# A hybrid attention and mixture-of-experts block: rotary dimensions gathered in one tile of q and one of k, and POOL's large operations given to DVE

## The chip, the cores and the metric

The kernel runs on one core of a Trainium2 chip. The metric is the device time of one execution in microseconds. In the profile the engines are PE (matrix products), PEld (loading their stationary operands), DVE (vector), ACT (scalar), POOL (GpSimd) and SP, which here only issues transfers.

## The reference

One encoder layer over 1024 tokens of width 1024, in float32. The part that the change touches is the input projection of the first sub-layer:

```python
mod = jax.nn.silu(c) @ w_ada[l] + b_ada[l]
sh1, sc1, g1, sh2, sc2, g2 = jnp.split(mod, N_MOD, axis=-1)
h = rms_norm(x, norm1_g[l]) * (1.0 + sc1[:, None]) + sh1[:, None]
z = h @ w_in[l]
q = z[..., :A].reshape(B, S, N_DIFF_HEADS, 2, DIFF_HEAD_DIM)
k = z[..., A:2 * A].reshape(B, S, N_DIFF_HEADS, 2, DIFF_HEAD_DIM)
v = z[..., 2 * A:3 * A].reshape(B, S, N_DIFF_HEADS, DIFF_VALUE_DIM)
u = z[..., 3 * A:].reshape(B, S, N_POOL_GROUPS, POOL_GROUP_DIM)
a_out = diff_attention(q, k, v, lam, subln_g[l], lambda_init)
p_out = multiscale_pool(u, w_pool[l], pool_scale[l])
```

A is 512, and there are four heads with two components of 64 dimensions each, so eight components for q and eight for k. In each component the first 16 dimensions are rotated: the first 8 and the next 8 are paired, t1·cos − t2·sin and t2·cos + t1·sin. The other 48 pass unchanged. q is scaled by 0.125. `multiscale_pool` takes means over windows of 2, 4, 8 and 16 tokens, one for each group of 128 channels, subtracts the input, and multiplies by a 128x128 matrix. After this sub-layer come a second norm, routing to 2 of 32 experts, the experts, a gated residual and a final norm.

## The kernel before

Activations lie transposed: channels on the 128 partitions, the 1024 tokens along the row. A **slab** is a 128x1024 float32 buffer; 50 of them go round (`slab`). Every precise product is made of three float32r products, high·high, low·high and high·low (`mm3`), so each operand is split: ACT writes the high half (`AF.Copy` to float32r), and DVE or POOL writes the low half as operand minus high (`split`). Nearly all instructions go through one helper line, L82, so they are told apart by tile names. All engines run in program order; the order is that in which the code is written.

The stage around the change is the projection, some 244 us of the span. It does, interleaved:

- `norm1`, `norm1_high`, `norm1_rest`, `norm1_low` for the 8 row blocks k of x: multiply by the root (`xt`), apply scale and shift on ACT (`hh` and `xt`), low half `hl`.
- `wa_sum` and `mod_row`: 48 products of a 128x1024 slab of the modulation weights (`wt`) with the vector `cB`, summed along the row, on DVE.
- 16 projection tiles in the order of ORDER, 48 matrix products of 128x512 each (`pz_q`, `pz_k`, `pz_v`, `pz_u`, in `project`). Tiles 0 to 2 are computed together, block by block, as `hh` and `hl` come (`project3`); tiles 3 to 15 follow one after another. The loop over m runs, for each tile: load weights two tiles ahead (`win`), split those one tile ahead (`wih` on ACT, `wil` on DVE), project, hand the result to a generator (`rope`, `pool_mix`, `values`), take up to three more `mod_row`, and from m = 7 split one slab of the output projection (`wo`, `woh`). `run_later` moves the generators of earlier tiles on by a step.
- `rope` for the four q and four k tiles, one per head: ACT takes the tile from PSUM (`zq`, `zk`), DVE swaps the 8-row halves (`zp`), then two products with `rope_c` and `rope_s`, a sum and the split, on POOL, except for the first product and the split of q0 and k0. The halves go to DRAM (`qd`, `kd`).
- `pool_mix` for the four u tiles: ACT takes the tile (`ub`), POOL makes the running sums (`us`, and on both row ends `ends`), DVE corrects the ends and subtracts, PE multiplies (`py`), ACT and DVE split (`muh`, `mul`).
- from tile 12 on, the first scores of the attention (`s`), their row maxima (`mx`) and exponentials (`e`), before the tile's own products.

PSUM for the tiles is a ring of two 128x1024 buffers (`pt`, tag "p"), which the scores share. SP issues the transfers in order; each waits also for the transfer issued eight before it. `stack_load` brings a head's q and k back, each half stacked as the products want it, at m = 9 and 10 for head 0, and in `attend` for heads 1 to 3.

Of the kernel before, what the change touches and what calls it, by code (L numbers as in the profile page):

```python
# [29 lines left out]
PAD = 8  # L30
# [5 lines left out]
SQ_MAX = float(np.finfo(np.float32).max) * TINY ** 2  # L36
LOAD = 28
AHEAD = 4
ORDER = ["q0", "k0", "v0", "q1", "k1", "u3", "v1", "u2", "q2", "k2", "u1", "q3", "k3", "u0", "v2", "v3"]
START = 12  # L40
STEP = "S0 T0 P0 d1 x1 H0 M0 O L C D0 X0 S1 T1 P1 H1 M1 o Q"
LOADS = {n: 1 for n in range(20, 30)}
# [7 lines left out]
ROWS = [5, 8, 11, 13]  # L50
MODS = {0: 1, 1: 2, 2: 2, **{m: 3 for m in range(3, 12)}}
WO = 7
ROPE = {"q0": "cl", "k0": "cl"}
STACK = (9, 10, 14)
FIRST = (16 - START) // 2
ML = 6
# [12 lines left out]
def block_kernel(ctx: ExitStack, tc: tile.TileContext, A):  # L69
# [4 lines left out]
    dram = ctx.enter_context(tc.tile_pool(name="dram", bufs=1, space=bass.MemoryType.DRAM))  # L74
# [27 lines left out]
    def dma(dst, src):  # L102
        tc.keep_in_program_order(nc.sync.dma_start(dst, src))
# [47 lines left out]
    xt = []  # L151
    for k in range(KD):
        t = slab(f"xt{k}")
# [27 lines left out]
                       allow_small_or_imprecise_dtypes=True)  # L181
    wr = cst.tile([P, KD, 36], F32, name="wr")

    qd = dram.tile([NH, 2, P, S], F32, name="qd")
    kd = dram.tile([NH, 2, P, S], F32, name="kd")
    vd = dram.tile([NH, 2, P, S], F32, name="vd")
    mxd = dram.tile([2, 2, 2, P, 2, 512], F32, name="mxd")
    wod = dram.tile([KD, 2, P, D], F32, name="wod")
# [22 lines left out]
    with tc.tile_pool(name="ps0", bufs=2, space=PSUM) as psum, tc.tile_pool(name="ps1", bufs=2, space=PSUM) as psum1, \  # L211
# [64 lines left out]
        for k in range(KD):  # L276
            sq = slab(f"sq{k}") if k else ssq
# [21 lines left out]
        prs = rows(pt("prs"), r8)  # L299
        rstd = slab("rstd")  # L300
        wa_sum(1, 0)
        w_split(0, pool)
        wa_add(0)
        wa_sum(1, 1)
        act.activation(rstd, prs, AF.Copy)
# [2 lines left out]
        hh, hl = [], []  # L308

        def norm1(k):  # L310
            (pool if k % 2 else dve).tensor_tensor(xt[k], xt[k], rstd, op=OP.mult)

        def norm1_high(k):
            hh.append(slab(f"hh{k}", dt=F32R))
# [4 lines left out]

        def norm1_low(k):  # L320
            hl.append(slab(f"hl{k}", dt=F32R))
            (pool if k % 2 else dve).tensor_tensor(hl[k], xt[k], f(hh[k]), op=OP.subtract)

        rope_c, rope_s = slab("rope_c"), slab("rope_s")
        wpe = slab("wpe", (576,))
# [17 lines left out]
                if 1 in parts:  # L343
                    pe.matmul(PZ[m][h], hi[:, k], hl[k][:, cs], start=False, stop=(k == KD - 1))

        shuf = [(i + 8) % 16 if i < 16 else i for i in range(32)]

        def pool_mix(g, pz):

            w = WINDOWS[g]  # L350
            cur = u = slab(f"ub{g}")
            act.activation(u, pz, AF.Copy)
            ends = sm("ends", (2, 16 + PAD))
            pool.memset(ends, 0.0)
            for i, c in enumerate((0, S - 16)):
                pool.tensor_copy(ends[:, i, PAD - PAD * i:16 + PAD - PAD * i], u[:, c:c + 16])
            lo, hi, size, n = 0, 0, 1, 0
            while size < w:
                a, b = max(1, size // 2), size // 2
                lo, hi = lo + a, hi + b  # L360
                nx, ne = slab(f"us{g}_{n}"), sm("ends", (2, 16 + PAD))
                for y, x, e in ((nx, cur, S - hi), (ne, ends, 16 + PAD - hi)):
                    pool_tt(y[..., lo:e], x[..., lo - a:e - a], x[..., lo + b:e + b], OP.add)
                cur, ends, size, n = nx, ne, size * 2, n + 1
            yield
            yield
# [12 lines left out]
            yield
            for x, t in enumerate((hi, lo)):  # L380
                for a in range(2):
                    dma(mxd[x, a, g // 2, :, g % 2], f(t[:, a * 512:(a + 1) * 512]))

        def rope(nm, pz):
            h = int(nm[1])
            z = slab("z" + nm)
            act.activation(z, pz, AF.Copy, scale=0.125 if nm[0] == "q" else 1.0)
            zp = slab("zp_" + nm)
            dve.stream_shuffle(zp, z, shuf)
            (dve if "c" in ROPE.get(nm, "") else pool).tensor_tensor(z, z, rope_c, op=OP.mult)  # L390
            pool_tt(zp, zp, rope_s, OP.mult)
            pool_tt(z, z, zp, OP.add)
            yield
            hi, lo = slab("th" + nm, dt=F32R), z.bitcast(F32R)
            split(z, hi, lo, None if "l" in ROPE.get(nm, "") else pool)
            yield
            for x, t in enumerate((hi, lo)):
                if nm[0] == "k":
                    dma(kd[h, x], f(t))
                else:  # L400
                    for j in range(2):
                        dma(qd[h, j, 64 * x:64 * x + 64], f(t[64 * j:64 * j + 64]))
# [90 lines left out]
        def stack_load(h, part):  # L493

            q, k1, k2, v = ST.setdefault(h, ([], [], [], []))
            if part == 2:
                for x in range(2):
                    v.append(slab(f"v{x}_{h}", (T, P), F32R))
                    dma(f(v[x].rearrange("p a b -> p (a b)")), vd[h, x])
                return  # L500
            q.append(slab(f"sq{h}_{part}", dt=F32R))
            dma(f(q[-1]), qd[h, part])
            for lab, dst, x in (("k1", k1, 0), ("k2", k2, 1)):
                dst.append(slab(f"{lab}_{h}_{part}", dt=F32R))
                for c in range(2):
                    dma(f(dst[-1][64 * c:64 * c + 64]), kd[h, x, 64 * part:64 * part + 64])

        SUM, MXS, E, WT, PW, SQ, SS8, MX = ({} for _ in range(8))
        Y8 = cst.tile([P, NH, T], F32, name="Y8")
# [170 lines left out]
                    for h in range(2):  # L680
                        project(m, h, (k,), (lo,))

        for k in (0, 1, 3):
            norm1(k)
        w_split(1)
        for k in range(KD):
            if k > 1:
                wa_add(k)
            norm1_high(k)
            if k == 1:  # L690
                w_split(2)
            norm1_rest(k)
            for n in {0: (2,), 1: (3,), 2: (4, 5), 4: (6, 7)}.get(k, ()):
                wa_sum(n, 0)
                wa_sum(n, 1)
            norm1_low(k)
            if k + 2 + 2 * (k % 2) < KD:
                norm1(k + 2 + 2 * (k % 2))
            if k == 0:
                project3(0, (0, 1))  # L700
            elif k == 1:
                project3(0, (2,))
            if k:
                project3(k, (0, 1, 2))
            if k >= 6:
                w_split(k - 3)
        done = 0
        for m, nm in enumerate(ORDER):
# [15 lines left out]
                project(m, 1, range(KD))  # L724
            pz = PZ.pop(m)
            pz = PF[m] if m != 2 else pz
            g = {"u": pool_mix, "v": values}[nm[0]](int(nm[1]), pz) if nm[0] in "uv" else rope(nm, pz)
            next(g, None)
            if m == 15:
                combine(FIRST - 1)  # L730
# [532 lines left out]
def _layouts(inp):  # L1263
    g = {k: np.asarray(v) for k, v in inp.items()}
    a = {}
# [71 lines left out]
```

## Time and profile before

| | |
|---|---|
| median of 3 runs | 1204.95 us (1195.96 to 1205.28) |
| profiled execution | 1198.64 us, span of the trace 1196.9 us |
| busy | PE 1105.3 us (92% of the span), DVE 1014.7, ACT 732.4, POOL 396.8 |
| transfers | 349.60 MB, mean 292 GB/s |

The profiled execution lies within the three runs, 6.3 us below their median. Times of the trace are counted from the start of its span. A PE that is busy is not always a PE at full speed: the granted clock stands beside it in the windows.

### The profile page before, as it was taken

To read this page: it belongs to the slowest core of one execution; us is meant where nothing else is said; L and a number is where in the kernel's file an instruction comes from. 1 tells how busy PE (TensorE), PEld (TensorE's weight loads), DVE (VectorE), ACT (ScalarE), POOL (GpSimd) and SP (SyncE) were. 2 spreads that over 40 slices of the span, in tenths; PEclk is the share of its full clock that TensorE was granted. 3 is DMA by queue.
4 is the path that set the end of the run, shared out by engine and by line. 5 is a ranking of instruction groups with operands and counts; after the bars stand their busy time and mean duration, and the time that the engine had idled before them with its cause. 6 is when DMAs were issued, how large, how long until landed. Compare 5 with 4: busy or idle time off the path is not lost.

```text
span 1196.9 us, 15760 instructions
## 1 busy us (share of the span) xinstructions
PE 1105.3 (92%) x5319; PEld 903.4 (75%) x5319; DVE 1014.7 (85%) x1187; ACT 732.4 (61%) x937; POOL 396.8 (33%) x260
## 2 busy tenths in 40 slices
PE   6696989899999999988999999999999999999975
PEld 6485866677888887777788888888888888888742
DVE  5969898868999725899899999999999999999927
ACT  5443222248888600222788888888888888888812
POOL 3546977737888600343111011011111111101001
PEclk8698999899999999977999999999999999999988
DMA  9836499489563784566699999999999999999155
GB/s 369 314 116 241 125 397 323 174 296 278 136 188 108 299 312 161 164 243 245 197 363 380 383 380 391 392 388 387 384 386 384 388 382 384 384 387 380 46 211 220
DMA packets 102950, 349.60 MB, mean 292 GB/s; under 512 B 15986, under 2 KB 16914, under 8 KB 102866
## 3 DMA queue, kind: packets, MB, share of 16 engines
q1 hardware_dynamic: 91266, 323.08, 73.9%
q0 software_dynamic: 11456, 24.96, 5.6%
q8 instruction: 43, 0.70, 0.2%
q10 hardware_dynamic: 144, 0.52, 0.1%
q14 instruction: 41, 0.34, 0.1%
HBM read 309.95 MB, written 55.33 MB: 305 GB/s over the span
## 4 chain that ended last, share of the span: by engine, by line
issue 46%; PE 26%; DVE 16%; POOL 6%; DMA 4%; ACT 1%; SPq 0%; POOLq 0%; DVEq 0%; ACTq 0%
PE pm L82 7%; PE s L82 4%; DVE wt L82 4%; PE po L82 4%; POOL x L82 4%; PE pz_v L82 3%; POOL yd L82 2%; PE pz_u L82 2%; PE pw L82 2%; DVE rt L82 2%; DMA wt<-in_w_ada 2%; DVE fy L82 1%; PE yp L82 1%; DVE wil L82 1%; DVE xn L82 1%
## 5 line engine op out<-in xcount | busy, mean ns | idle before, releaser
L82 DVE TENSOR_TENSOR wl<-we,wh 128x1024 fp32r<-128x1024 f32 x384 | 458.4, 1222 | 39.6 <-ACT wh L82 34.4
L82 ACT ACTIVATE wh<-we 128x1024 fp32r<-128x1024 f32 x384 | 399.7, 1058 | 60.5 <-PE pg L82 29.0
L82 PE MATMUL pg<-wh,xs 128*128 128x512 f32 x1024 | 338.8, 397 | 0.0
L82 PEld LDWEIGHTS pg<-wh,xs 128*128 128x128 f32 x1024 | 192.8, 188 | 39.1 <-ACT xs L82 0.2
L82 PE MATMUL pg<-wl,xs 128*128 128x512 f32 x512 | 200.0, 391 | 0.0
L82 POOL DMA_INDIRECT yd<-y,ix x32 | 32.1, 1004 | 479.6 <-ACT y L82 466.9
L82 PE MATMUL py<-wh,hth 128*128 128x512 f32 x512 | 171.9, 397 | 1.0 <-ACT hth L82 0.7
L82 PEld LDWEIGHTS py<-wh,hth 128*128 128x128 f32 x512 | 96.1, 188 | 21.8 <-DVE hth L82 1.2
L82 PEld LDWEIGHTS pg<-wl,xs 128*128 128x128 f32 x512 | 96.7, 189 | 18.2
L82 PE MATMUL py<-wl,hth 128*128 128x512 f32 x256 | 99.9, 390 | 0.0
L82 ACT ACTIVATE e<-s,mx 128x1024 f32<-128x1024 f32 x64 | 71.6, 1119 | 42.6 <-DVE mx L82 40.3
L82 DVE SCALAR_TENSOR_TENSOR wt<-wt,cB 128x1024 f32<-128x1024 f32 x48 | 91.1, 1943 | 0.8 <-ACT cB L82 0.8
L82 PE MATMUL s<-k,sq 128*128 128x512 f32 x256 | 74.0, 412 | 10.4 <-ACT e L82 10.3
L82 DVE TENSOR_REDUCE mx<-s 128x1 f32<-128x1024 f32 x64 | 78.2, 1221 | 6.0 <-PE s L82 3.2
L82 POOL TENSOR_TENSOR e<-e,e 128x1024 f32<-128x1024 f32 x32 | 76.5, 2390 | 2.7
L82 PE MATMUL po<-wh,v 128*128 128x256 f32 x256 | 60.7, 301 | 0.0
L82 PEld LDWEIGHTS s<-k,sq 128*128 128x128 f32 x256 | 44.8, 193 | 19.6 <-ACT e L82 13.1
L82 POOL DMA_INDIRECT x<-xnd,ix x32 | 46.2, 1442 | 35.3 <-PE px L82 13.6
L82 PEld LDWEIGHTS py<-wl,hth 128*128 128x128 f32 x256 | 48.2, 188 | 9.4
L82 ACT ACTIVATE xn<-x 128x1024 f32<-128x1024 f32 x7 | 7.4, 1062 | 74.1 <-DVE x L82 68.8
L82 POOL TENSOR_SCALAR e<-e,cc 128x1024 f32<-128x1024 f32 x32 | 39.2, 1225 | 37.2 <-DVE cc L82 16.7
L82 DVE SCALAR_TENSOR_TENSOR x<-pm,Y,x 128x1024 f32<-128x1024 f32 (+1 forms) x33 | 41.2, 1249 | 7.8 <-PE pm L82 6.0
(227 smaller groups left out, 2035.8 us busy)
## 6 DMA issues: line engine op xcount, KB each, us to landing
we<-in_w_exp SPq DMA_DIRECT2D x384, 512.0 KB, 6.9
wt<-in_w_ada SPq DMA_DIRECT2D x48, 512.0 KB, 8.7
win<-in_w_in SPq DMA_DIRECT2D x16, 512.0 KB, 9.1
k<-kd SPq DMA_DIRECT2D x32, 256.0 KB, 9.4
woB<-wod SPq DMA_DIRECT2D x16, 512.0 KB, 6.0
fy<-yd SPq DMA_DIRECT2D x16, 512.0 KB, 10.1
xt<-in_xT SPq DMA_DIRECT2D x8, 512.0 KB, 7.7
wo<-in_w_out SPq DMA_DIRECT2D x8, 512.0 KB, 6.6
```

The source lines that it names most:

```text
L82: ins = getattr(self.eng, op)(*args, **kw)
```

## The change

The columns of w_in are put in another order on the host: the 16 rotated dimensions of all eight components of q make one tile, `qr`, those of k another, `kr`, and the 48 others of each component fill three tiles each (`q0` to `q2`, `k0` to `k2`). `rope` runs for `qr` and `kr` alone, all on DVE. The other six go through a new generator, `plain`, which splits them straight from PSUM. What POOL did in `norm1`, `norm1_low`, `w_split(0)` and `pool_mix` goes to DVE; POOL keeps one small memset for each u tile. `stack_load` puts a component together from 16 rows of one tile and 48 of others. The number of matrix products is the same.

```diff
-ORDER = ["q0", "k0", "v0", "q1", "k1", "u3", "v1", "u2", "q2", "k2", "u1", "q3", "k3", "u0", "v2", "v3"]
+ORDER = ["qr", "kr", "v0", "q0", "k0", "u3", "v1", "u2", "q1", "k1", "u1", "q2", "k2", "u0", "v2", "v3"]
+ROT = 16
...
         def norm1(k):
-            (pool if k % 2 else dve).tensor_tensor(xt[k], xt[k], rstd, op=OP.mult)
+            dve.tensor_tensor(xt[k], xt[k], rstd, op=OP.mult)
...
-            (pool if k % 2 else dve).tensor_tensor(hl[k], xt[k], f(hh[k]), op=OP.subtract)
+            dve.tensor_tensor(hl[k], xt[k], f(hh[k]), op=OP.subtract)
...
-                    pool_tt(y[..., lo:e], x[..., lo - a:e - a], x[..., lo + b:e + b], OP.add)
+                    dve.tensor_tensor(y[..., lo:e], x[..., lo - a:e - a], x[..., lo + b:e + b], op=OP.add)
...
+        def qk_store(nm, hi, lo):
+
+            d, i = (qd if nm[0] == "q" else kd), 0 if nm[1] == "r" else 1 + int(nm[1])
+            for x, t in enumerate((hi, lo)):
+                dma(d[x, i], f(t))
+
         def rope(nm, pz):
...
-            (dve if "c" in ROPE.get(nm, "") else pool).tensor_tensor(z, z, rope_c, op=OP.mult)
-            pool_tt(zp, zp, rope_s, OP.mult)
-            pool_tt(z, z, zp, OP.add)
+            dve.tensor_tensor(z, z, rope_c, op=OP.mult)
+            dve.tensor_tensor(zp, zp, rope_s, op=OP.mult)
+            dve.tensor_tensor(z, z, zp, op=OP.add)
             yield
             hi, lo = slab("th" + nm, dt=F32R), z.bitcast(F32R)
-            split(z, hi, lo, None if "l" in ROPE.get(nm, "") else pool)
...
+            split(z, hi, lo)
+            yield
+            qk_store(nm, hi, lo)
+
+        def plain(nm, pz):
+
+            hi, lo = slab("th" + nm, dt=F32R), slab("tl" + nm, dt=F32R)
+            if nm[0] == "q":
+                act.activation(hi, pz, AF.Copy, scale=0.125)
+                dve.scalar_tensor_tensor(lo, pz, 0.125, f(hi), op0=OP.mult, op1=OP.subtract)
+            else:
+                split(pz, hi, lo)
...
-            q.append(slab(f"sq{h}_{part}", dt=F32R))
-            dma(f(q[-1]), qd[h, part])
-            for lab, dst, x in (("k1", k1, 0), ("k2", k2, 1)):
-                dst.append(slab(f"{lab}_{h}_{part}", dt=F32R))
-                for c in range(2):
-                    dma(f(dst[-1][64 * c:64 * c + 64]), kd[h, x, 64 * part:64 * part + 64])
+            c = 2 * h + part
+            for lab, dst, d, xs in (("sq", q, qd, (0, 1)), ("k1", k1, kd, (0, 0)), ("k2", k2, kd, (1, 1))):
+                t = slab(f"{lab}{h}_{part}", dt=F32R)
+                dst.append(t)
+                for i, x in enumerate(xs):
+                    r = d[x].rearrange("a p s -> (a p) s")
+                    dma(f(t[64 * i:64 * i + ROT]), r[ROT * c:ROT * c + ROT])
+                    n = P + (64 - ROT) * c
+                    dma(f(t[64 * i + ROT:64 * i + 64]), r[n:n + 64 - ROT])
```

Three places show how the order on the engines moves. First DVE at the start of the stage, from the first normalised block (`xt_72` is block 0, `xt_74` block 1, `hl_304` or `hl_303` the low half of block 0; the numbers only tell buffers apart). Before:

```order
L82 TENSOR_TENSOR xt_72<-xt_72,rstd 128x1024
L82 TENSOR_TENSOR wil_296<-win_154,wih_295 128x1024
L82 SCALAR_TENSOR_TENSOR wt_2_156,gs<-wt_2_156,cB 128x1024
L82 SCALAR_TENSOR_TENSOR wt_2_158,sh<-wt_2_158,cB 128x1024
L82 TENSOR_TENSOR hl_304<-xt_72,hh_299 128x1024
L82 TENSOR_TENSOR xt_76<-xt_76,rstd 128x1024
L82 TENSOR_TENSOR wil_324<-win_160,wih_323 128x1024
```

After:

```order
L82 TENSOR_TENSOR xt_72<-xt_72,rstd 128x1024
L82 TENSOR_TENSOR xt_74<-xt_74,rstd 128x1024
L82 TENSOR_TENSOR wil_295<-win_154,wih_294 128x1024
L82 SCALAR_TENSOR_TENSOR wt_2_156,gs<-wt_2_156,cB 128x1024
L82 SCALAR_TENSOR_TENSOR wt_2_158,sh<-wt_2_158,cB 128x1024
L82 TENSOR_TENSOR hl_303<-xt_72,hh_298 128x1024
L82 TENSOR_TENSOR xt_76<-xt_76,rstd 128x1024
L82 TENSOR_TENSOR wil_323<-win_160,wih_322 128x1024
L82 SCALAR_TENSOR_TENSOR wt_3_252,gs<-wt_3_252,cB 128x1024
L82 SCALAR_TENSOR_TENSOR wt_3_254,sh<-wt_3_254,cB 128x1024
L82 TENSOR_TENSOR hl_329<-xt_74,hh_320 128x1024
L82 TENSOR_TENSOR xt_78<-xt_78,rstd 128x1024
```

Each odd block's product and low half, which stood on POOL, now stand between DVE's own.

Second DVE between the low halves of the weights of tile 6 and of tile 7, around tile 5 (`u3`). Before, to the weights of tile 7 (`wil_840`):

```order
L82 TENSOR_TENSOR wil_746<-win_661,wih_745 128x1024
L82 SCALAR_TENSOR_TENSOR wt_3_653,mcol<-wt_3_653,cB 128x1024
L82 SCALAR_TENSOR_TENSOR wt_4_656,mcol<-wt_4_656,cB 128x1024
L82 SCALAR_TENSOR_TENSOR wt_5_659,mcol<-wt_5_659,cB 128x1024
L82 TENSOR_TENSOR mcol<-mcol,cols 128x8
L82 TENSOR_TENSOR wil_840<-win_743,wih_839 128x1024
```

After, the first twelve rows; a third `wt`, `mcol` and the low half for tile 7 follow:

```order
L82 TENSOR_TENSOR wil_737<-win_658,wih_736 128x1024
L82 COPY ends<-ub_789 128x16 x2
L82 TENSOR_TENSOR us_0_795<-ub_789 128x1023
L82 TENSOR_TENSOR ends<-ends 128x2x23
L82 TENSOR_TENSOR us_1_799<-us_0_795 128x1021
L82 TENSOR_TENSOR ends<-ends 128x2x21
L82 TENSOR_TENSOR us_2_803<-us_1_799 128x1017
L82 TENSOR_TENSOR ends<-ends 128x2x17
L82 TENSOR_TENSOR us_3_807<-us_2_803 128x1009
L82 TENSOR_TENSOR ends<-ends 128x2x9
L82 SCALAR_TENSOR_TENSOR wt_3_650,mcol<-wt_3_650,cB 128x1024
L82 SCALAR_TENSOR_TENSOR wt_4_653,mcol<-wt_4_653,cB 128x1024
```

The running sums now stand in DVE's queue ahead of three `wt` and the weights of the next tile but one, and their first instruction waits for `ub`, which ACT writes when tile 5 is done.

Third SP at m = 9, where q and k of head 0's first component come back. Before, with the load and the store behind them:

```order
L103 DMA sq_0_1194<-qd 128x1024
L103 DMA k_0_0_1196<-kd 64x1024 x2
L103 DMA k_0_0_1199<-kd 64x1024 x2
L103 DMA win_1202<-in_w_in 128x1024
L103 DMA qd<-thq_1176 64x1024 x2
```

After:

```order
L103 DMA sq_0_1171<-qd 16x1024
L103 DMA sq_0_1171<-qd 48x1024
L103 DMA sq_0_1171<-qd 16x1024
L103 DMA sq_0_1171<-qd 48x1024
L103 DMA k_0_1176<-kd 16x1024
L103 DMA k_0_1176<-kd 48x1024
L103 DMA k_0_1176<-kd 16x1024
L103 DMA k_0_1176<-kd 48x1024
L103 DMA k_0_1181<-kd 16x1024
L103 DMA k_0_1181<-kd 48x1024
L103 DMA k_0_1181<-kd 16x1024
L103 DMA k_0_1181<-kd 48x1024
```

Five transfers of 256 to 512 KB have become twelve of 64 and 192 KB with the same bytes in all; the weights of tile 12 (`win`) come behind them as before.

## Rows read from the trace of the kernel before

**Rows 1.** Window of the stage: length, busy us of PE, PEld, DVE, ACT, POOL, PE clock.
```profile
26.80:271.00 244.20, 205.50 (x829) 162.46 (x830) 207.65 (x193) 82.47 (x105) 156.71 (x71) 0.90 0.71 251
```

**Rows 2.** Waits of PE, 26.8 to 271 us: total us, times, longest.
```profile
PE pz_q L82 <- DVE hl L82: 11.5, 2, 8.1
PE pz_u L82 <- DVE wil L82: 8.4, 2, 5.0
PE s L82 <- ACT e L82: 5.7, 2, 3.3
...
PE prow L82 <- DVE mcol L82: 2.6, 1, 2.6
PE pz_q L82 <- DVE wil L82: 2.6, 1, 2.6
```

**Rows 3.** Timeline of DVE, 105 to 125 us: start, duration, instruction, [idle before it <-releaser].
```profile
110.78 1.22 DVE L82 SCALAR_TENSOR_TENSOR wt<-wt,cB 128x1024 f32<-128x1024 f32 x1
...
111.92 1.22 DVE L82 TENSOR_TENSOR wil<-win,wih 128x1024 fp32r<-128x1024 f32 x1
...
118.71 3.41 DVE L82 SCALAR_TENSOR_TENSOR wt<-wt,cB 128x1024 f32<-128x1024 f32 x1
```

**Rows 4.** Timeline of POOL, the same stretch.
```profile
117.65 3.38 POOL L82 TENSOR_TENSOR zp_k<-zp_k,rope_s 128x1024 f32<-128x1024 f32 x1
```

**Rows 5.** Groups of DVE, 26.8 to 271 us: xcount | busy us, mean ns | idle before.
```profile
L82 DVE SCALAR_TENSOR_TENSOR wt<-wt,cB 128x1024 f32<-128x1024 f32 x44 | 86.3, 2009 | 0.0
...
L82 DVE TENSOR_TENSOR wo<-wo,woh 128x1024 fp32r<-128x1024 f32 x8 | 16.4, 2055 | 10.6 <-ACT woh L82 10.6
...
L82 DVE TENSOR_TENSOR vl<-pv,vh 128x512 fp32r<-128x512 f32 x6 | 3.9, 684 | 2.9 <-ACT vh L82 2.9
```

**Rows 6.** Timeline of DVE: first normalised slab, first rotation.
```profile
26.82 1.23 DVE L82 TENSOR_TENSOR xt<-xt,rstd 128x1024 f32<-128x1024 f32 x1 [3.68 <-ACT rstd L82]
...
79.52 1.35 DVE L82 STREAM_SHUFFLE zp_q<-zq 128x1024 f32<-128x1024 f32 x1
```

**Rows 7.** Timeline of PE: end of tiles 0 to 2, start of tile 5.
```profile
78.70 0.61 PE L82 MATMUL pz_v<-hl,wih 128*128 128x512 f32 x2
...
113.19 0.80 PE L82 MATMUL pz_u<-hh,wil 128*128 128x512 f32 x1 [5.01 <-DVE wil L82]
```

**Rows 8.** Windows of tiles 6, 10, 11, 13, 14; the last columns: PE clock, DMA share, GB/s.
```profile
125.70:136.70 11.00, 11.00 (x51) 9.01 (x49) 11.00 (x11) 2.92 (x3) 10.93 (x7) 1.00 0.70 202
175.84:189.37 13.53, 13.53 (x48) 10.93 (x49) 12.37 (x7) 2.01 (x2) 12.19 (x4) 0.78 1.04 333
194.06:206.50 12.44, 12.44 (x47) 10.06 (x48) 11.32 (x11) 2.00 (x2) 9.28 (x5) 0.86 1.02 303
225.14:239.11 13.97, 13.97 (x52) 11.36 (x53) 11.83 (x8) 3.96 (x5) 11.48 (x4) 0.84 0.15 38
243.43:256.81 13.38, 13.38 (x53) 10.83 (x54) 10.41 (x14) 6.18 (x8) 7.08 (x6) 0.88 1.02 376
```

**Rows 9.** Chain of work, in order of time: the end of the last projection tile.
```profile
265.32 5.47 PE pz_v L82 x24
```

**Rows 10.** Waits of SP's own queue, 26.8 to 310 us.
```profile
SPq L103 <- POOL ends L82: 45.5, 4, 17.1
```

**Rows 11.** Timeline of SP: loads of q and k of heads 1 and 2.
```profile
274.65 0.43 SPq L103 DMA_DIRECT2D sq<-qd  x1
275.13 2.47 SPq L103 DMA_DIRECT2D k<-kd  x4
...
296.62 5.62 SPq L103 DMA_DIRECT2D k<-kd  x4
```

**Rows 12.** Timeline of DVE: first row maxima of head 1 and of head 2.
```profile
297.97 1.23 DVE L82 TENSOR_REDUCE mx<-s 128x1 f32<-128x1024 f32 x1
...
334.77 1.21 DVE L82 TENSOR_REDUCE mx<-s 128x1 f32<-128x1024 f32 x1
```

**Rows 13.** Tile k (scores of queries and keys): its loads, from issue to landing.
```profile
DMA to landing us min/median/max: 5.7/9.4/12.7
```

More of the change, by code (lines that the diff above doesn't have):

```diff
@@ L52 @@
 WO = 7
-ROPE = {"q0": "cl", "k0": "cl"}
 STACK = (9, 10, 14)
@@ L182, in block_kernel @@
     wr = cst.tile([P, KD, 36], F32, name="wr")
-    qd = dram.tile([NH, 2, P, S], F32, name="qd")
-    kd = dram.tile([NH, 2, P, S], F32, name="kd")
+    qd = dram.tile([2, 4, P, S], F32, name="qd")
+    kd = dram.tile([2, 4, P, S], F32, name="kd")
     vd = dram.tile([NH, 2, P, S], F32, name="vd")
@@ L301, in block_kernel @@
         wa_sum(1, 0)
-        w_split(0, pool)
+        w_split(0)
         wa_add(0)
@@ L344, in project @@
                     pe.matmul(PZ[m][h], hi[:, k], hl[k][:, cs], start=False, stop=(k == KD - 1))
-        shuf = [(i + 8) % 16 if i < 16 else i for i in range(32)]
+        shuf = [16 * (i // 16) + (i + 8) % 16 for i in range(32)]
         def pool_mix(g, pz):
@@ L355, in pool_mix @@
             for i, c in enumerate((0, S - 16)):
-                pool.tensor_copy(ends[:, i, PAD - PAD * i:16 + PAD - PAD * i], u[:, c:c + 16])
+                dve.tensor_copy(ends[:, i, PAD - PAD * i:16 + PAD - PAD * i], u[:, c:c + 16])
             lo, hi, size, n = 0, 0, 1, 0
@@ L382, in pool_mix @@
                     dma(mxd[x, a, g // 2, :, g % 2], f(t[:, a * 512:(a + 1) * 512]))
+        def qk_store(nm, hi, lo):
+            d, i = (qd if nm[0] == "q" else kd), 0 if nm[1] == "r" else 1 + int(nm[1])
+            for x, t in enumerate((hi, lo)):
+                dma(d[x, i], f(t))
         def rope(nm, pz):
-            h = int(nm[1])
-            z = slab("z" + nm)
+            z, zp = slab("z" + nm), slab("zp_" + nm)
             act.activation(z, pz, AF.Copy, scale=0.125 if nm[0] == "q" else 1.0)
-            zp = slab("zp_" + nm)
             dve.stream_shuffle(zp, z, shuf)
-            (dve if "c" in ROPE.get(nm, "") else pool).tensor_tensor(z, z, rope_c, op=OP.mult)
-            pool_tt(zp, zp, rope_s, OP.mult)
-            pool_tt(z, z, zp, OP.add)
+            dve.tensor_tensor(z, z, rope_c, op=OP.mult)
+            dve.tensor_tensor(zp, zp, rope_s, op=OP.mult)
+            dve.tensor_tensor(z, z, zp, op=OP.add)
             yield
             hi, lo = slab("th" + nm, dt=F32R), z.bitcast(F32R)
-            split(z, hi, lo, None if "l" in ROPE.get(nm, "") else pool)
+            split(z, hi, lo)
             yield
[L397 to L402, printed above, removed]
+            qk_store(nm, hi, lo)
[7 more added lines that the diff above has]
+            yield
+            qk_store(nm, hi, lo)
         def values(h, pz):
@@ L681, in project3 @@
                         project(m, h, (k,), (lo,))
-        for k in (0, 1, 3):
+        for k in (0, 1):
             norm1(k)
@@ L696, in block_kernel @@
             norm1_low(k)
-            if k + 2 + 2 * (k % 2) < KD:
-                norm1(k + 2 + 2 * (k % 2))
+            if k + 2 < KD:
+                norm1(k + 2)
             if k == 0:
@@ L726, in block_kernel @@
             pz = PF[m] if m != 2 else pz
-            g = {"u": pool_mix, "v": values}[nm[0]](int(nm[1]), pz) if nm[0] in "uv" else rope(nm, pz)
+            if nm[0] in "uv":
+                g = {"u": pool_mix, "v": values}[nm[0]](int(nm[1]), pz)
+            else:
+                g = (rope if nm[1] == "r" else plain)(nm, pz)
             next(g, None)
@@ L1288, in _layouts @@
     a["w_ada"] = np.ascontiguousarray(wa.reshape(6, D, KD, P).transpose(0, 2, 3, 1))
-    wi = g["w_in"][0].reshape(KD, P, 4, 4, P)
-    wi = np.stack([wi[:, :, "qkvu".index(nm[0]), int(nm[1])] for nm in ORDER])
+    wi = g["w_in"][0].reshape(KD, P, 4, 512)
+    split = {}
+    for i, nm in enumerate("qk"):
+        c = wi[:, :, i].reshape(KD, P, 8, 64)
+        split[nm] = np.concatenate([c[..., :ROT].reshape(KD, P, P), c[..., ROT:].reshape(KD, P, 3 * P)], axis=2)
+    for i, nm in enumerate("vu"):
+        split[nm] = wi[:, :, 2 + i]
+    place = lambda nm: P * (0 if nm[1] == "r" else int(nm[1]) + (nm[0] in "qk"))
+    wi = np.stack([split[nm[0]][:, :, place(nm):place(nm) + P] for nm in ORDER])
     a["w_in"] = np.ascontiguousarray(wi.transpose(0, 2, 1, 3))
@@ L1296, in _layouts @@
     rope = np.zeros((2, P, S), np.float32)
-    rope[0] = 1.0
-    for c in (0, 64):
+    for c in range(0, P, ROT):
         rope[0, c:c + 8] = cs
```

## Prediction

> **What bounds the kernel now.** I read the stage's window first. From 26.8 to 271 us PE is busy 205.50 of 244.20 us at a mean granted clock of 0.90, DVE 207.65, POOL 156.71 [rows 1]. The reader is to see that PE has work all the time here and still loses some 39 us of idle time, and more at the lower clock, while DVE is nearly always busy. The view of waits names who is late: PE waits 11.5 us for `hl`, 8.4 and 2.6 us for `wil`, 2.6 us for `mcol`, all DVE, and 5.7 us for `e`, which stands behind a DVE row maximum [rows 2]. ACT is busy for 82.47 us only [rows 1].
>
> Then the two timelines side by side. A 128x1024 operation of DVE with two operands in SBUF takes 1.22 us, the next one starting 1.14 us after it, as long as POOL is quiet [rows 3]. The same operation takes 3.41 us when it starts inside a POOL product, and that product takes 3.38 us [rows 3, 4]. So the two share something, and both pay. The groups show how often: the 44 modulation products average 2.01 us instead of 1.22, the eight low halves `wo` 2.06 [rows 5]. The 512-wide low halves whose operand is in PSUM keep 0.68 us, so an operand from PSUM is not slowed [rows 5].
>
> SP's queue has its own victim: it stood 45.5 us, 17.1 at the longest, in waits put down to POOL [rows 10], mostly stores of halves that POOL had not made, with loads behind them.
>
> **The change part by part.** DVE gains 29 operations of 1024 columns (eight for norm1, one for w_split(0), ten running sums, ten net for q and k), 18 small ones and loses six shuffles of 1.35 us [rows 6]. At 1.14 us [rows 3] that is 29 x 1.14 + 18 x 0.2 − 6 x 1.35 = about +29 us. Without POOL the 44 `wt` alone give back 44 x (2.01 − 1.22) = 35 us, and the rest of DVE's large operations about as much again. So DVE's total falls by about 45 us; what counts is its chain at three places. Where the trace has no row for an operation of the new kernel, I take the nearest: a low half from PSUM is two `vl`, 1.4 us [rows 5]; the small sums of 18 to 46 columns between 0.1 and 0.4 us, of which I take 0.2.
>
> (A) Tiles 0 to 2. DVE starts at 26.82 in both [rows 6]; the extra `wil` of tile 0 falls into the 3.68 us of idle time before that. In the new order `hl` of block 4 is the 25th large operation from there: 26.82 + 25 x 1.14 = 55.3. PE then has 6 products of that block and 18 each of blocks 5 to 7, 60 in all. A tile of 48 takes 11.0 us [rows 8], so 60 take 13.8, and the tiles end at 69.1, if the later `hl` come every 1.1 to 2.3 us, as the order has them. Before they ended at 78.70 + 0.61 = 79.3 [rows 7]. Gain 10.2 us.
>
> (B) Start of tile 5, which needs its `wil`. Before: 113.19 [rows 7]. After: the first shuffle starts 0.2 us after the tiles' end, as before (79.52 [rows 6]), so at 69.3. From there DVE has 18 large operations (20.5 us), two shuffles (2.7), two `vl` (1.4), the small chain for lambda (1.5 to 4) and some 0.7 us of dependent starts: 27 to 29 us, end at about 97. PE's tiles 3 and 4 end at 92, so PE still waits for DVE, some 4 us. Total gain at this point 16.2 us, A included.
>
> (C) Tiles 5 to 15, which ended at 265.32 + 5.47 = 270.8 [rows 9]. In this stretch PE waits 3.4 (8.4 − 5.0), 2.6, 2.6 and 5.7 us [rows 2], in sum 14.3. After each of these waits the clock is at its lower level for a while: tiles 10 and 11 (less one matmul, 10.8 us at full clock) took 13.53 and 12.44, tiles 13 and 14 with their scores (some 11.9) took 13.97 and 13.38, at granted clocks of 0.78 to 0.88 where an undisturbed tile has 1.00 [rows 8]. That is 2.7 + 1.6 + 2.1 + 1.5 = 7.9 us. If DVE's work for a tile fits under PE's 11 us, all 22.2 go. It just about fits. After a pooling tile DVE waits for `ub` (about 1 us after the tile's end), and behind that wait stand the sums, three `wt` and the next `wil`: for the first, 8 large and 7 small operations, 10.5 us, ready 11.5 us after the tile's end against 11.0. The eight waits for ACT's `woh` (10.6 us in sum [rows 5]) stay. I count 1.1 us of such overhangs. One wait is new: `plain` keeps its PSUM buffer until DVE has made the low half, so tile 12 must wait for `tlq2` where it waited for ACT alone; some 1.4 us. Net 22.2 − 2.5 = 19.7 us.
>
> Sum at the end of the projection: 16.2 + 19.7 = 35.9 us. What follows is bound by PE and moves forward unchanged, but for one thing.
>
> (D) The loads of q and k. A head's ten transfers become 24. Head 0's come long before tile 12. For heads 2 and 3 a head's work is 334.77 − 297.97 = 36.8 us [rows 12]. Tight is head 1: issued from 274.65 [rows 11], its second half wanted about 2 us after 297.97 [rows 12]. At 2.47/4 = 0.62 us each [rows 11] the last is issued at 289.5 and lands a median 9.4 us later, 12.7 at the most [rows 13]: 298.9 to 302.2, against 300. Bounds 0 and, if the pieces come a fifth more slowly, 5 us; I take 1.5, between the median's 0 and the longest landing's 2.2.
>
> The trace shows four such loads issued in 2.47 us while each needs 9.4 to land, so several are under way at once. [...]
>
> Forecast: 1198.64 (the profiled execution, whose span is 1196.9) − 35.9 + 1.5 = 1164.2. That execution lies 6.3 us below the median of the three runs, which spread over 9.3, and I cannot tell which of these the new kernel will draw; I go a quarter of that way: 1166.
>
> **The rivals.**
>
> Rival 1, DVE and SP stay late in part. Each of the four pooling tiles now puts an in-order wait and 5 to 10 us of sums ahead of the next `wil`. For it speaks that (C) leaves less than 1 us of room per tile, and that any wait of 2 to 3 us brings the lower clock with it (2 us more each, as in [rows 8]). Against it: half of the tiles leave DVE 3 to 6 us free. Price: four tiles with 2 + 2 us, or 16 us of the 35.9; time 1182.
>
> Rival 2, slower: the pieces. If a piece occupies SP for c us, heads 1 to 3 bring 24c − 15 + 2 x (26c − 37) us of stalls. With the worst spacing in the trace, 5.62/4 = 1.4 [rows 11], head 1 loses about 19 and the others nothing, and the kernel still gains. From c = 1.64 on the 36 us are used up; at 2.0 the stalls are 63 us: 1198.64 − 35.9 + 63 = 1226. Against it: 0.62 in an idle queue, and the slow four waited for free buffers.
>
> Rival 3, POOL is not what slows DVE. Then 29 operations at 2.0 us come on top, some 50 us of DVE work net, and the stage grows by some 10 to 20: 1213. The 1.22 and 3.41 of one operation 8 us apart speak against it [rows 3].
>
> **How the numbers follow.** Forecast 0.70, rival 1 0.20, rival 2 0.04, rival 3 0.03, and 0.03 for a gain of under 10 us by something unseen. The forecast's own range is 1154 (all waits gone, at the low end of the runs' spread) to 1175. Reaching over most of rival 1 gives 1154 to 1186. One per cent, 12 us, is about what a measurement of this kernel can tell from no change. Faster by over 1%: 0.70 + 0.20 + 0.02 of rival 2 = 0.92. Within 1%: 0.03. Slower: 0.05.
>
> **What would show it.** In the new trace, DVE's `wt` should average 1.2 us and POOL be nearly empty before the first `e`. The last `pz_v` should end near 235. Tile 5 should start near 97, after a wait of about 4 us, and the first shuffle near 69. Waits of PE for `wil` over 2 us after the u tiles would be rival 1; waits of PE for loads of q or k beyond 5 us, rival 2; `wt` still near 2 us, rival 3. The prediction is wrong if something on SP, a store or a free buffer, now ends last in the stage, which I could only follow in the order, not in time.

## The result and the profile after

The changed kernel takes 1163.43 us, median of four runs (1162.43 to 1168.21), where the kernel before took 1202.9 us in the runs beside it: ratio 0.9689, 95% interval 0.9638 to 0.974. The prediction was 1166 with a range of 1154 to 1186. The profiled execution took 1163.77 us, its span is 1162.0.

The window of the stage, the counterpart of [rows 1], with the same columns:

```profile
26.80:235.00 208.20, 197.35 (x830) 157.15 (x831) 158.07 (x227) 76.02 (x97) 5.40 (x6) 0.96 0.81 294
```

The reader is to see that DVE does more (227 operations for 193) in less time (158.07 us for 207.65), that POOL has gone from 156.71 us to 5.40, and that PE's own time fell by 8 us (205.50 to 197.35) while its waits fell from 39.7 us to 12.9 and the granted clock of the stage went from 0.90 to 0.96.

DVE's groups in the stage (as [rows 5]), and then, from DVE's and PE's timelines, the places where the prediction set its marks ([rows 6, 7]):

```profile
L82 DVE SCALAR_TENSOR_TENSOR wt<-wt,cB 128x1024 f32<-128x1024 f32 x44 | 51.5, 1219 | 0.0
```

```profile
25.80 2.36 DVE L82 TENSOR_TENSOR xt<-xt,rstd 128x1024 f32<-128x1024 f32 x2 [2.02 <-ACT rstd L82]
...
68.54 1.36 DVE L82 STREAM_SHUFFLE zp_qr<-zqr 128x1024 f32<-128x1024 f32 x1
```

```profile
67.73 0.61 PE L82 MATMUL pz_v<-hl,wih 128*128 128x512 f32 x2
...
94.83 0.50 PE L82 MATMUL pz_u<-hh,wil 128*128 128x512 f32 x1 [3.08 <-DVE wil L82]
```

The 44 `wt` take 1.22 us each where they took 2.01. Tiles 0 to 2 end at 68.3, tile 5's `wil` is used at 94.8. The waits of PE in the stage (as [rows 2]), 39.7 us in all before, are now all of these, 12.9 us:

```profile
PE pz_qr L82 <- ACT hh L82: 3.6, 1, 3.6
PE pz_u L82 <- DVE wil L82: 3.1, 1, 3.1
PE pz_qr L82 <- DVE hl L82: 2.4, 3, 1.1
PE pz_k L82 <- DVE tlq L82: 1.5, 1, 1.5
PE s L82 <- ACT e L82: 1.1, 1, 1.1
PE pz_u L82 <- DVE tlk L82: 1.0, 1, 1.0
PE pz_q L82 <- ACT zqr L82: 0.2, 1, 0.2
```

Windows of tiles 5, 10, 11, 13 and 14 (as [rows 8], but tiles 13 and 14 without their scores; the granted clock stands third from the end), and the end of the last tile in the chain of work (as [rows 9]):

```profile
94.83:107.41 12.58, 12.58 (x48) 10.26 (x49) 5.64 (x8) 0.00 (x0) 0.00 (x0) 0.86 1.01 357
...
153.72:164.70 10.98, 10.98 (x50) 9.10 (x49) 8.55 (x13) 3.04 (x3) 0.00 (x0) 1.00 1.00 324
165.92:176.82 10.90, 10.90 (x49) 8.82 (x48) 9.76 (x15) 3.19 (x4) 0.14 (x1) 1.00 1.02 341
194.44:207.08 12.64, 12.63 (x49) 10.35 (x50) 5.96 (x7) 3.21 (x4) 0.00 (x0) 0.88 1.03 417
209.73:220.63 10.90, 10.90 (x51) 8.88 (x50) 8.88 (x15) 3.22 (x4) 1.73 (x1) 1.00 0.84 310
```

```profile
229.00 5.47 PE pz_v L82 x24
```

Of tiles 3 to 15 only 5 and 13 still run at the lower clock in part, 0.86 and 0.88 where the others have 1.00. Both begin after a wait, of 3.1 and 1.0 us; tile 12 does too, 1.5 us, and keeps 1.00. In a second profile of the same kernel (e8 below) tile 13 keeps it as well, 11.2 us at a granted clock of 1.00, behind waits of 0.8 and 1.0 us. The projection ends at 234.5 instead of 270.8. What follows took 926.1 us and takes 927.5.

One stretch of the chain of work of the changed kernel goes another way than I had it:

```profile
172.60 7.69 DMA sq<-qd
...
181.59 5.91 DMA win<-in_w_in
```

These are the second half of head 0's small loads and, issued behind them, the weights of tile 13. DVE's `wil` of tile 13 waits for them, behind it stands the row maximum, behind that ACT's `e`: the wait of 1.1 us at 192.3. The wait of 1.0 us at 194.4 follows it but has another reason: tile 13 needs the PSUM buffer of tile 12, which `plain` keeps until DVE has made `tlk`.

### The profile page after: what moved, and what is told of

It reads as the page before. It is cut to its first block, busy times and chain, and to the rows that moved or that the text cites. A ratio compares the mean times of both kernels' runs of the same rounds, so it can differ in the third digit from the quotient of the medians.

```text
span 1162.0 us, 15763 instructions
## 1 busy us (share of the span) xinstructions
PE 1094.0 (94%) x5319; PEld 894.8 (77%) x5319; DVE 967.5 (83%) x1222; ACT 726.8 (63%) x931; POOL 242.7 (21%) x195
## 4 chain that ended last, share of the span: by engine, by line
issue 46%; PE 27%; DVE 12%; POOL 6%; DMA 6%; ACT 1%; SPq 1%; POOLq 0%; DVEq 0%; ACTq 0%
PE pm L82 6%; PE s L82 4%; PE po L82 4%; POOL x L82 4%; PE pz_v L82 3%; PE pz_u L82 3%; POOL yd L82 2%; PE pw L82 2%; DVE rt L82 2%; DVE wt L82 2%; DMA k<-kd 1%; DVE fy L82 1%; SPq L103 1%; PE yp L82 1%; PE pz_q L82 1%
## 5 line engine op out<-in xcount | busy, mean ns | idle before, releaser
L82 DVE SCALAR_TENSOR_TENSOR wt<-wt,cB 128x1024 f32<-128x1024 f32 x48 | 56.3, 1219 | 0.8 <-ACT cB L82 0.8
L82 PE MATMUL pm<-woB,mxh 128*128 128x512 f32 x128 | 44.5, 430 | 4.4 <-DVE x L82 4.4
```

Of the source, the lines that this page charges most:

```text
L82: ins = getattr(self.eng, op)(*args, **kw)
```

## The experiments

Two theories at first. A: what the change gains, it gains by taking POOL out of DVE's way; the new tiles only save DVE instructions. B: the new tiles are most of it. Two kernels do one half each.

**e1, old tiles, POOL's work on DVE**, in the kernel before.

```diff
-            (pool if k % 2 else dve).tensor_tensor(xt[k], xt[k], rstd, op=OP.mult)
+            dve.tensor_tensor(xt[k], xt[k], rstd, op=OP.mult)
...
-            pool_tt(z, z, zp, OP.add)
+            dve.tensor_tensor(z, z, zp, op=OP.add)
```

> The tiles of the kernel before, one per head, but everything large that POOL did in the stage (norm1, norm1_low, w_split(0), the sums of pool_mix, rope) is done by DVE. Beside the changed kernel DVE has 24 more products and sums and 6 more shuffles, 24 x 1.14 + 6 x 1.35 = 35 us. Theory A (POOL out of DVE's way is most of the gain, the new tiles only save DVE instructions): wt at 1.22 us, tiles 0 to 2 end near 68 us as in the changed kernel, tile 5 starts about 5 us later than there, at 100, because q1's rotation stands ahead of its wil; DVE is 90% busy in the stage and PE waits for wil after the q and k tiles. Last pz_v near 245, time 1168 to 1180. Theory B (the new tiles are most of the gain): DVE with its 188 us of work in a stage of 208 cannot keep up, 1185 or more.

1177.34 us, ratio 0.9807 (0.978 to 0.9834). The `wt` average 1.219 us, DVE is busy for 188.65 us, and the last `pz_v` ends at 251.2, 6 us later than I expected; the time lies in the range of theory A. The waits of PE in the stage, the largest first:

```profile
PE pz_u L82 <- DVE wil L82: 6.8, 3, 3.5
PE s L82 <- ACT e L82: 4.9, 3, 3.3
```

**e2, new tiles, POOL's work left on POOL** in the norm, `w_split(0)`, the sums and two operations of each rotation, in the changed kernel.

```diff
-            dve.tensor_tensor(hl[k], xt[k], f(hh[k]), op=OP.subtract)
+            (pool if k % 2 else dve).tensor_tensor(hl[k], xt[k], f(hh[k]), op=OP.subtract)
...
-                    dve.tensor_tensor(y[..., lo:e], x[..., lo - a:e - a], x[..., lo + b:e + b], op=OP.add)
+                    pool_tt(y[..., lo:e], x[..., lo - a:e - a], x[..., lo + b:e + b], OP.add)
```

> The new tiles, but POOL keeps what it had in norm1, norm1_low, w_split(0), pool_mix and in the rotation (the second product and the sum). POOL then has about 80 us of large operations in the stage instead of 157. Theory A: DVE's operations beside POOL's are slow again, most of all up to 80 us; tiles 0 to 2 end at 76 to 80 instead of 67.4, wt averages 1.5 to 1.8 us, waits of PE for hl come back; time 1174 to 1184. Theory B: most of the gain stays, 1164 to 1170.

1175.2 us, 0.9787 (0.976 to 0.9813). Tiles 0 to 2 end where they did in [rows 7], and `hl` is what PE waits for. PE's timeline, PE's waits, DVE's groups:

```profile
78.86 0.61 PE L82 MATMUL pz_v<-hl,wih 128*128 128x512 f32 x2
```

```profile
PE pz_qr L82 <- DVE hl L82: 11.7, 2, 8.1
```

```profile
L82 DVE SCALAR_TENSOR_TENSOR wt<-wt,cB 128x1024 f32<-128x1024 f32 x44 | 68.5, 1605 | 0.0
```

Both times lie where theory A put them, but its "most" is too strong: beside the 1200.33 us of before, e1 gains 23.0 and e2 25.1, and the two halves together about 37. Each alone gives some two thirds, since fewer instructions of DVE and faster ones shorten the same queue. The split is not clean: the new tiles also take rotations from POOL, which in e2 is busy for 75.8 us of the stage and not for 156.7, and so `wt` is faster there too, 1.61 us for 2.01. Step A of the prediction is the half that e2 lacks.

**e3 and e4, idle work for POOL.** They ask rival 3's question directly, in the changed kernel.

```diff
         for m, nm in enumerate(ORDER):
+            if m > 3:
+                wd = [f(x).rearrange("p a b -> p (a b)") for x in wsp[m]]
+                for _ in range(3):
+                    pool.tensor_tensor(rstd, wd[0], wd[1], op=OP.add)   # e3
+                    pool.tensor_copy(rstd, wd[1])                       # e4
```

> The changed kernel with three POOL additions of two 128x1024 operands in SBUF for each of tiles 4 to 15, which nothing in the computation uses (they write into the slab of rstd, which is done with by then). Theory A: each takes 3.4 us beside DVE and keeps DVE from 2.2 us of its own work (one operation in 3.4 us instead of three in 3.6), 36 x 2.2 = 79 us in all. DVE has about 40 us to spare from tile 4 on, so the stage grows by some 35 to 45 us, and wt averages 2 us or more: 1195 to 1215. Rival 3 of the prediction (POOL is not what slows DVE): 1163 to 1167 and wt at 1.22 us.

> The same 36 idle POOL operations, but copies: one operand read in place of two. If any large POOL operation on SBUF slows DVE, as above, 1185 to 1210 with wt near 2 us. If it is the second operand that they share, wt stays at 1.22 us and the time at 1163 to 1168. In the attention of the changed kernel POOL's one-operand e<-e,cc takes 1.20 us, no more than DVE's own operations, which speaks for the second: 1165.

e3: 1191.31 us in its one run, 28 us lost, a little less than theory A had it (1195 to 1215), and `wt` averages 1.55 us in the stage where I had said 2 or more. DVE is busy for 207.2 us to the end of the projection, 49.2 more than in the changed kernel, 1.37 for each addition and not 2.2. From 26.8 to 235 us DVE is idle for 24.3 us of e3 and busy for another 15 with an operand from PSUM; that part of the additions ran there is my estimate. Rival 3 is ruled out: nothing but POOL was added. The additions also hold the slabs of the weights a little longer, but so do the copies of e4, which cost nothing. DVE's timeline and POOL's, the same stretch of e3:

```profile
129.32 3.40 DVE L82 SCALAR_TENSOR_TENSOR wt<-wt,cB 128x1024 f32<-128x1024 f32 x1
...
132.66 3.41 DVE L82 TENSOR_TENSOR wil<-win,wih 128x1024 fp32r<-128x1024 f32 x1
...
141.12 1.21 DVE L82 TENSOR_TENSOR us<-ub 128x1023 f32<-128x1023 f32 x1
142.25 2.40 DVE L82 TENSOR_TENSOR ends<-ends 128x46 f32<-128x46 f32 x1
144.57 1.21 DVE L82 TENSOR_TENSOR us<-us 128x1021 f32<-128x1021 f32 x1
```

```profile
128.39 6.60 POOL L82 TENSOR_TENSOR rstd<-wih,wil 128x1024 f32<-128x1024 f32 x2
...
136.21 8.38 POOL L82 TENSOR_TENSOR rstd<-wih,wil 128x1024 f32<-128x1024 f32 x3 [1.15 <-DVE wil L82]
```

In these rows the two take turns, instruction by instruction, where DVE reads two operands from SBUF: DVE starts its second operation 3.34 us after the first, and POOL's two additions beside them take 3.30 us each. A sum over 46 columns, 0.20 us elsewhere, takes 2.40, as long as a whole POOL addition that runs alone (`e<-e,e` in the attention: 2.39 us), and the large `us` before and after it take 1.21. With one operand in SBUF it depends on the operation: in e3 the copies `ends<-ub` of 16 columns are held up too, 0.76 us on average for 0.17 elsewhere, while in the kernel before a shuffle that ran wholly beside a POOL addition, at 85.4 (the addition from 84.46 to 87.73), took 1.34 us, where the changed kernel's two average 1.35.

e4: 1163.94 us in its one run, as without the copies, but neither of the two answers that I had offered. DVE's and POOL's timelines in e4:

```profile
118.31 1.22 DVE L82 TENSOR_TENSOR wil<-win,wih 128x1024 fp32r<-128x1024 f32 x1
...
120.59 2.05 DVE L82 SCALAR_TENSOR_TENSOR wt<-wt,cB 128x1024 f32<-128x1024 f32 x1
```

```profile
119.66 5.86 POOL L82 COPY rstd<-wil 128x1024 f32<-128x1024 f32 x3 [12.88 <-DVE wil L82]
```

The copies take turns with DVE too, 1.95 us each here and an operation of DVE every 1.98, they are only short: 9.4 us of DVE in all (167.50 busy against 158.07), which fits into its idle time, 50.1 us in the changed kernel. So it is not the second operand of POOL's operation alone.

**e11, fills in their place**: `pool.memset(rstd, 0.0)` for the copy.

> The changed kernel with 36 idle POOL fills of a 128x1024 slab, which read nothing. In e3 and e4 a DVE operation and a POOL operation beside it took turns: an addition (2.39 us alone) made DVE's operation 3.4 us, a copy made it 2.05. If they share the reading of SBUF, DVE's operations beside the fills stay at 1.22 us and the time at 1162 to 1165. If any large POOL operation on SBUF takes its turn, those beside the fills take 2 us; with about 40 us to spare on DVE the time is then still 1163 to 1168, so the duration of wt beside the fills is what tells.

1165.23 us in one run. POOL's timeline and DVE's in e11, nine fills back to back:

```profile
113.91 9.07 POOL L82 MEMSET rstd<- 128x1024 f32 x9
```

```profile
114.92 1.22 DVE L82 SCALAR_TENSOR_TENSOR wt<-wt,cB 128x1024 f32<-128x1024 f32 x1
```

The 44 `wt` of this kernel average 1.218 us, in the changed kernel 1.219: the fills, which read nothing, cost DVE no time here.

**e5, the pieces doubled.** It prices step D and rival 2.

```diff
-                    dma(f(t[64 * i:64 * i + ROT]), r[ROT * c:ROT * c + ROT])
+                    for j in range(2):
+                        cs = slice(512 * j, 512 * j + 512)
+                        dma(f(t[64 * i:64 * i + ROT, cs]), r[ROT * c:ROT * c + ROT, cs])
...
```

> The changed kernel with each of the small loads of q and k cut in two along the row, 48 pieces for a head where there were 24, the same bytes. Theory A (a piece costs issue time on SP, and head 1 has no slack left): in the changed kernel head 1's 24 took 14 us to issue, 0.58 us each, and its first scores waited 1.1 us for k. 24 more at 0.32 (the median duration of one issue) to 0.58 us are 8 to 14 us, all of which head 1 waits for; heads 2 and 3 have 15 us to spare and wait for nothing. Head 0's pieces stand in front of the weights of tile 13 and delay its wil too, by up to 10 us. Sum 1172 to 1186. Theory B (what counts is the bytes, or pieces overlap fully): 1163 to 1166, and then the change could not lose by its pieces at all.

1174.23 us, 0.9772 (0.9751 to 0.9794): some 10 us lost, as theory A had it, but at the other place. The last `pz_v` ends at 241.45, 7.0 us later, and what follows takes 930.05 us, 2.5 more. SP's timeline and PE's in e5:

```profile
176.07 6.64 SPq L103 DMA_DIRECT2D sq<-qd  x8
...
182.82 7.33 SPq L103 DMA_DIRECT2D k<-kd  x16
190.50 0.35 SPq L103 DMA_DIRECT2D win<-in_w_in  x1
```

```profile
200.06 2.08 PE L82 MATMUL s<-k,sq 128*128 128x512 f32 x4 [9.38 <-ACT e L82]
```

The weights of tile 13 are issued at 190.5 instead of 181.6, and the scores ahead of tile 13 wait for 9.4 us. Head 1's 48 pieces, 0.5 us each, cost PE 0.7 us of waits for k. Behind them a store of `vl` is issued at 271.3 only, and DVE's `wl` waits 2.0 us for it at 280. So the pieces are paid for by what is queued behind them on SP more than by the head that they belong to.

**e6, e7, e8: the waits that are left.** e6 moves four `wt` out of the way of tile 5's `wil`. e7 moves the chain for lambda too, spreads the `wt` by DVE's load, and puts the weights of tiles 12 and 13 ahead of head 0's loads. e8 is the changed kernel beside them.

```diff
-MODS = {0: 1, 1: 2, 2: 2, **{m: 3 for m in range(3, 12)}}
+MODS = {0: 1, **{m: 3 for m in range(3, 12)}, 12: 4}                    # e6
+MODS = dict(enumerate([1, 1, 1, 2, 3, 2, 4, 2, 4, 4, 1, 3, 4]))        # e7
...
-            if m > 2 and m + 2 < 16:
+            if m > 2 and m + 2 < 16 and m not in (10, 11):              # e7
...
-            if m == 3:
+            if m == 6:                                                  # e7
                 lamt = slab("lamt", (4, 64))
...
+            if m in (9, 10):                                            # e7
+                w_load(m + 3)
```

> The changed kernel with four of the modulation products (wt) moved from tiles 1 and 2, where they stand ahead of tile 5's wil, to tile 12. Theory A (step B: DVE's queue sets the start of tile 5): wil is ready 4 x 1.14 = 4.6 us earlier, the wait of 3.1 us is gone, tile 5 starts at 91.8 instead of 94.8 and loses nothing to a lower clock; 1159 to 1161. Rival: the wait only moves, since DVE has 4.6 us more to do at tile 12, ahead of the weights and the row maximum for tiles 13 and 14: 1163 to 1166.

> The changed kernel with three things moved: three of the wt ahead of tile 5 and the small chain for lambda to later tiles, fewer wt at the tiles with running sums and more at the others, and the loads of the weights of tiles 12 and 13 put ahead of head 0's small loads on SP. If the waits left in the stage are what the trace says (3.1 us for wil at tile 5, 1.5 for tlq2, 1.1 and 1.0 around tile 13 behind the late weights, and 1 to 1.5 us of lower clock behind them): 6 to 8 us, 1156 to 1158. If head 0's small loads don't hold up tile 13's weights, its waits stay: 1159 to 1161.

> The changed kernel itself, beside the others on the same chip: 1162 to 1165.

e6 1163.61, e7 1163.77, e8 1164.1; ratios 0.9682, 0.9686 and 0.9682, each known to about 0.002. No gain from either, and my expectations for both failed; the rival of e6 had the time, but put it down to DVE. SP's timeline and PE's in e6 show why:

```profile
173.01 8.60 SPq L103 DMA_DIRECT2D k<-kd  x8
181.72 0.37 SPq L103 DMA_DIRECT2D win<-in_w_in  x1
```

```profile
191.32 2.08 PE L82 MATMUL s<-k,sq 128*128 128x512 f32 x4 [5.29 <-DMA wod<-wo]
```

The wait at tile 5 is gone, and PE waits at tile 13 instead: its weights, issued at 181.7 as before, set the start of those scores at 191.3, however early PE comes (192.3 in the changed kernel). (The releaser that the row names landed by chance then; in between stand ACT's `wih`, `wil`, the row maximum and `e`.) In e7 tile 13 starts at 188.8, but now the weights and the `wo` slab for the next step stand behind the same loads: DVE waits 3.45 us for `wo`, and the scores ahead of tile 14 wait 3.6.

**e9, e10, e12: head 0's loads earlier.** Head 0 needs only `qr`, `kr`, `q0` and `k0`, so its loads can go out at tiles 6 and 7. e9 does this in the changed kernel, e10 in e7, e12 also issues the loads of heads 1 to 3 one attention step earlier.

```diff
-STACK = (9, 10, 14)
+STACK = (6, 7, 14)
...
-            if live(n) and its[n][1] == 3 and its[n][0] + 1 < NH:
+            if live(n) and its[n][1] == 2 and its[n][0] + 1 < NH:       # e12
```

> The changed kernel with head 0's small loads of q and k at tiles 6 and 7 instead of 9 and 10. Head 0 needs only the tiles qr, kr, q0 and k0 in the new layout, which are stored by then, and at 130 to 142 us the transfers are at 0.43 of their time against 0.97 to 1.03 from 142 to 207. Theory A (the 24 pieces on SP, 10 us for each half, hold up the weights of tile 13): wil of tile 13 no longer waits, the waits of 1.1 and 1.0 us around it and the lower clock of that tile (12.6 us instead of 11.9) go, 2 to 3 us: 1160 to 1162. Rival: the pieces hold up the weights of tiles 8 and 9 instead, or six slabs held longer stall the other loads: 1164 to 1170.

> The same in the kernel of e7_all_waits, whose tile 13 started 5.6 us earlier than in the changed kernel and whose end of the projection was only 1.5 us earlier, because the weights of tile 14 came behind the second half of head 0's loads. Theory A: now all of it arrives, 5 to 7 us, 1156 to 1159. Rival: transfers, busy for 0.9 to 1.0 of the time from tile 8 to 13, or the row maxima on DVE become the bound: 1160 to 1164.

> The kernel of e10_head0_early_all with the loads of heads 1 to 3 issued one attention step earlier, about 2 to 4 us. If step D's remainder (a wait of 1.1 us for k at head 1, and the scores behind it) is one of late issue, that wait goes and the time is 1155 to 1157. Rival: the slabs are not free or the transfers, at 1.0 of their time around 234 to 270 us, take it back: 1157 to 1162.

e9 1161.7 us, 0.9686 (0.9662 to 0.9711): the projection ends 3.0 us earlier, at 231.5, but the ratio doesn't tell it from no change. The wait of 1.1 us is gone; the one for `tlk`, which theory A also counted as won, stays at 1.3. e10 1156.85 us, 0.9646 (0.962 to 0.9672), its five runs of 1155.22 to 1158.62 all below the nine of the changed kernel: it beats both kernels. e12 1157.3 us, no further gain. PE's timeline in e10 shows no wait over 0.2 us at tile 5, and the granted clock from 94.8 to 107.4 us, most of tile 5, is 1.00, where the changed kernel has 0.86; its window of the stage, to the end of the last tile:

```profile
26.80:228.05 201.25, 193.90 (x829) 154.45 (x830) 159.10 (x227) 75.31 (x96) 4.95 (x6) 0.97 0.82 304
```

e7 alone moves its waits to tile 14, and e9 alone leaves the 3.1 us at tile 5; their projections end 1.5 and 3.0 us earlier than in the changed kernel. Both together take 6.4 us from the stage, and that is what the waits had promised in e7.

## Why the prediction was right

**The cause** was DVE's queue, as each step assumed: POOL's reading operations had stretched it, and e3 brings the slow operations back, 3.40 us for 1.22, by adding POOL work alone; the new tiles take instructions out of it (e1 against the changed kernel, 14 us). The waits of SP that were put down to POOL, the prediction's other victim [rows 10], are gone in the changed kernel; in e3 they come to 0.6 us, and it loses 28 us all the same. So they are not needed for such a loss; what they cost by themselves in the kernel before, no run shows.

**(A)** Predicted end of tiles 0 to 2 at 69.1, a gain of 10.2 us; measured 68.3, gain 11.0. DVE's first `xt` starts anywhere from 25.4 to 27.1 us in the executions of the kernels here; from that start it was 42.3 us predicted and 42.5 measured.

**(B)** Predicted 97 after a wait of 4 us; measured 94.8 after 3.1. The gain was 18.4 us and not 16.2: 0.8 us is the earlier first shuffle, 68.54 and not 69.3, the rest a queue of DVE of 26.2 us where I had 27 to 29.

**(C)** Predicted 19.7 us, measured 157.6 − 139.6 = 18.0. The waits of 14.3 us fell to 3.6, not to 2.5 (10.7 us). In the four tiles the clock gave back some 6 of the 7.9 us: about 2.7, 1.6 and 1.6 at tiles 10, 11 and 14 (there 13.38 against 10.90 and 0.93 for its scores), but next to nothing at tile 13 (13.97 against 12.64 and 1.20). The rest, 1 us or so, lies in tiles that I did not itemise. The wait for `tlq2` came as predicted (1.4; it was 1.53). The overhangs after the pooling tiles did not come. In their place stand two waits that the step lacked. The 1.0 us for `tlk` is the same keeping of a PSUM buffer by `plain`, one tile later; it stays in e9 and e10, 1.3 and 1.0 us. The 1.1 us for `e` comes from the late weights: step D said that head 0's loads "come long before tile 12", which is true of the data, and left out the weights of tile 13 that are issued behind them. It is also the prediction's own sign of being wrong, in part: at tile 13 it is a load queued on SP that comes last.

**(D)** Predicted 1.5 us at head 1; the rest after the projection did grow by 1.4, but not for that. Head 1's first scores do not wait. The only wait put down to k stands ahead of the first scores of head 2, in PE's timeline after:

```profile
297.21 1.20 PE L82 MATMUL s<-k,sq 128*128 128x512 f32 x4 [1.08 <-DMA k<-kd]
```

(In my expectations for e5 and e12 I had taken it for head 1's.) Head 2's loads had been issued by 274; the load that is named was issued at 293.4 and is one of head 3's. The same products wait as long in the kernel before, where ACT's `e` is named ([rows 12] have the row maximum that follows, at 334.77), and in e12, where it is `e` again. First the kernel before, then e12:

```profile
333.43 1.20 PE L82 MATMUL s<-k,sq 128*128 128x512 f32 x4 [1.08 <-ACT e L82]
```

```profile
290.60 1.19 PE L82 MATMUL s<-k,sq 128*128 128x512 f32 x4 [1.00 <-ACT e L82]
```

So D was 0, and a load landed just then by chance. The 1.4 us are covered by two later waits that the change doesn't touch and that grew by 1.0 us each: `yp` for `fy` 6.6 us after 5.5, `pm` 4.4 after 3.4 (2.3 in e12 and 5.3 in e8, so it varies by itself).

The sum of 35.9 us for the projection met 36.3, as two errors of about 2 us cancelled, and 1164.2 for the profiled execution met 1163.77. That is luck: from DVE's first `xt` to the end of the projection the same kernel took 208.7 us in this profile and 206.6 in that of e8. The 1.8 us added toward the median of before were not needed.

**The rivals.** Rival 1's waits for `wil` after the pooling tiles are absent, and so are rival 2's waits for loads of q or k; at 0.5 us a piece SP stays far from the break-even of 1.64, and no run shows the 2.0 at which that rival was priced. e5 shows where rival 2 was half right: pieces do cost, 0.3 us each for head 0's 24 more (7.0 us), through the weights behind them. SP issued head 1's 48 in 24 us, from 245.3 to 269.5, some 0.5 us apart. In the chain of work of e5 the piece of k issued at 269.1 lands 2.2 us later, so the pieces overlap.

## What to carry to other kernels

Work moved from POOL to DVE can shorten DVE's time, in e1 with the tiles as they were from 207.65 us to 188.65: where both read operands in SBUF, look whether a POOL operation costs DVE time before you call it free (an addition of e3 cost 1.37 us, a copy of e4 0.26, a fill of e11 nothing that shows), and compare one operation's duration with and without its neighbour rather than the busy shares. When a wait is removed, look for the next chain that is already due at about the same time (here the in-order queue of transfers); in this kernel two were due within a few microseconds, and removing one moved the end of the projection by 1.5 us (e7) or 3.0 (e9), removing both by 6.4 (e10). And price small transfers by what is queued behind them: e5's projection ended 7.0 us later that way.

## What the runs showed of the hardware

In e3, where both read SBUF and DVE reads two operands there, POOL and DVE do not share a rate, they alternate in whole instructions: a DVE sum over 46 columns takes 2.40 us, 0.20 without POOL's additions. Beside these, of which one takes 2.39 us alone, a DVE operation of two SBUF operands starts 3.34 us after the one before and is shown with 3.40 us, 2.2 more than its 1.22 alone, so its duration contains most of the other engine's instruction. Beside the POOL copies of e4 (1.08 us alone, 3.25 us for three) it starts every 1.98 and is shown with 2.05. DVE operations that read PSUM keep their times in e3 (`mul` 0.74 and `mx` 1.21 us, in the changed kernel 0.74 and 1.22), and so do DVE's groups beside the fills of e11 (`wt` and `wil` 1.22 us in both). What makes the two engines alternate no run shows.
